# A hybrid attention and expert layer on one core: 188 tokens gathered in five parts and 324 dense (before: 184 in four and 328), query weights' low parts on GpSimd, twenty early rows, three branch products ahead

## The chip, the cores and the metric

The kernel runs on one core of a Trainium2 chip. The time is the device time of one execution in microseconds (us), from the run itself; the median of several is given, with the lowest and the highest. Each kernel is also executed once under the hardware profiler; that execution has a time of its own.

Engines are named as in the profile: PE is TensorE (PEld its weight loads), DVE is VectorE, ACT is ScalarE, POOL is GpSimd, and SP is SyncE, which here only issues DMAs. L246 is line 246 of the kernel before.

## The reference

One layer over 16 meta tokens and 512 frames of width 2048, in float32: two attention mixers, whose gated outputs are added, and then a layer of 16384 experts, of which every token uses 128.

```python
hn = rmsnorm(h, norm_mix_g)
c_q, c_kv, k_rope, q_sb, k_sb, v_sb, gate_a, gate_b = split(hn @ w_in)
y_a = mla_attention(...)                 # 8 heads, softmax, chunk-causal
y_b = stick_breaking_attention(...)      # 8 heads
h += (sigmoid(gate_a) * (y_a @ w_branch_a) + sigmoid(gate_b) * (y_b @ w_branch_b)) @ w_out

x = rmsnorm(h, norm_ffn_g)
q = (x @ w_q).reshape(tokens, 8, 2, 128)             # 8 heads, two halves
s = einsum('thcd,hcnd->thcn', q, sub_keys)           # 128 keys for each half
s1, i1 = top_k(s[:, :, 0], 16);  s2, i2 = top_k(s[:, :, 1], 16)
top_s, pos = top_k(s1[..., :, None] + s2[..., None, :], 16)   # 16 of 256 pairs
idx = i1[...] * 128 + i2[...]                        # at pos
g = softmax(top_s)
act = g * gelu(einsum('tkd,td->tk', u[idx], x))      # 128 experts a token
h += einsum('tk,tkd->td', act, v[idx])
out = rmsnorm(h, final_norm_g)[frames]
```

## The kernel before

**Products.** Every float32 product is made of three matmuls (`mm3`, L258): both operands are split into a high part (`wh`, `xh`: a copy on ACT rounded to the type fp32r) and a low part (`wl`, `xl`: the operand minus its high part, on DVE by default), and low times high, high times low and high times high are added in PSUM. `wtile` (L232) does this for a weight tile of 128 x 1024: SP loads it (`wr`, four buffers), ACT copies the high part, and DVE, or the engine given as `eng`, subtracts the low part; `wh` and `wl` have three buffers. `front(name, m, hf, eng)` is `wtile` for the weights ahead of the expert layer. `split` (L263) is the same for other operands.

**Stages**, in program order: the projections of `w_in` and the stick-breaking heads; the eight MLA heads, whose generators `mla_s`, `mla_p` and `mla_y` are run in turns by `run`, so that one head's scores, another's projections and a third's output products alternate; the branch stage, 16 columns of `wa` and `wb` products with gates, which begins by splitting the stick-breaking output `yb` into `yh_b` and `yl_b`; `wo`; the query stage (16 columns `hc`, L1125), in which each column is one half of one head's query for all 512 tokens, two weight tiles of eight products each, followed by the scores against 128 keys and the top 16 of them for four token blocks (`top16`, L917 to L921: MAX, MAX_INDEX, MATCH_REPLACE on DVE; tiles `sc`, `wk`, `lists`); the u stage (128 steps `e`, L1347, each two weight tiles of eight products); the v stage (256 blocks in the order STEPS, L1441); and the final norm.

**Dense and gathered tokens.** The expert layer is computed in two ways. For ND = 328 tokens all 16384 experts are multiplied densely: in the u stage `u` times x, GELU, and a store to DRAM (`h_d`); in the v stage these come back (`hin`), are multiplied by a gate matrix from DRAM (`gin`; `g_d`, built during the u stage from the top-16 results) and multiplied with `v`. The other 184 tokens are gathered: for each of a token's 128 experts the row of `u` or `v` is fetched by an indirect DMA of 128 rows at once, and multiplied by DVE. These come in parts, NS = 128, 32, 16, 8: the first part is one token a partition and 128 gathers long; in a part of n tokens each token holds 128 / n partitions, and n gathers do. So the parts need 128 + 32 + 16 + 8 = 184 gathers of `u` and as many of `v`, 1 MB each. The x of the parts lie in `xg`, `xgb` and, reloaded from `xr_d`, in `lists`; the sums of the v rows of a part of n tokens are spread over its partitions and are added up at the end by matmuls with a selection matrix (`select`; `acc` is the output accumulator). For the last part 16 such matmuls of 128 x 8 stand in step 5 of the v stage (L1464 to L1469).

**Rows.** `todo` lists the gathers in their order. `send` issues the next one on POOL's queue (L1052) into a buffer `row`; `row_step` (L1057) sends what its lead asks for and then does one row on DVE: a multiply with a sum for `u` (L1065, 128 x 2048), a multiply-add for `v` (L1073). A NOSYNC dependency only keeps the row behind an earlier instruction of DVE (`mark`). In the query stage one row step is made at the end of every column from the sixth on (`if hc > 4`), 11 in all; two gathers are sent at the end of column 4. In the u stage `rows_due` keeps the number of rows done at the curve PACE: (0, 11), (14, 28), (60, 97), (127.5, 200). What remains is done in the v stage by PACE_V. In the query stage there are three `row` buffers, so a gather waits for the row step three before it.

These lines set the order around the rows and the query weights:

```python
1019 NU = 200
1023 PACE = (0, 14, 60, NK - 0.5), (11, 28, 97, NU)
1128 wh, wl = wq.pop((hc, hf)) if (hc, hf) in wq else front("wq", hc, hf, G if hf else V)
1155 split(qh, ql, ps)
1189 row_step(more["lo"], 2)
```

By L1128 the low parts of a column's second weight tile are on POOL and those of the first on DVE; (0, 0), (1, 0), (1, 1) and (2, 0), loaded ahead, are on DVE and (0, 1) is on POOL. POOL runs its queue in order, so there a low part stands behind the gathers issued before it.

## Time and profile before

| | us |
|---|---|
| median of three runs | 3459.06 (3458.64 to 3461.61) |
| profiled execution, its own time | 3459.31 |
| its span (first to last instruction) | 3457.6 |
| projections and stick-breaking heads | 0 to 800 |
| MLA heads | 800 to 965 |
| branch stage, then `wo` | 965 to 1148, 1148 to 1305 |
| query stage | 1305 to 1519 |
| u stage | 1519 to 2500 |
| v stage and final norm | 2500 to 3457 |

How to read the profile: the busy line gives each engine's busy time, its share of the span and its number of instructions. Below it the span is cut into 40 slices of 86 us, and a digit is the busy share in tenths. A group of instructions reads: line, engine, operation, output <- inputs, shapes, count | busy time, mean ns of one | idle time of the engine just before these instructions, and what ended most of it. Matmuls overlap, so that their mean is longer than the time from one to the next. A row of the waits names who waited with what, for whom with what, and then the total, the count and the longest. In the timeline and in the chain the first two numbers are start and duration. "x" counts merged instructions.

### The profile page before, as it was taken

The numbers are of one execution on the slowest core, as the hardware profiler recorded it, in microseconds if no ns is written. First come the engines' busy times: TensorE is split into PE (matmuls) and PEld (weight loads), VectorE is DVE, ScalarE is ACT, GpSimd is POOL, SyncE is SP. The second block draws the span as 40 slices with busy tenths as digits, with TensorE's granted clock in tenths as the row PEclk, the third lists the DMA queues.
The fourth block names the chain that finished last, engine by engine and source line by source line (L and its number), as shares of the span: only waits on it lengthen the run. The fifth ranks groups of instructions, "written<-read, shape, count | busy, mean of one in ns | idle before, by whom it ended". The sixth has DMA issues, their size and how long they took to land.

```text
span 3457.6 us, 53380 instructions
## 1 busy us (share of the span) xinstructions
PE 3420.5 (99%) x21115; PEld 3188.2 (92%) x21115; DVE 2573.5 (74%) x3573; ACT 1427.4 (41%) x2304; POOL 776.1 (22%) x555
## 2 busy tenths in 40 slices
PE   9999999999999999999999999999999999999997
PEld 8988888887888888889999999999999999999997
DVE  5533334445754557999999988887889999999997
ACT  4233333334543223223576776774333333333333
POOL 1000000000001113322333333333213333333320
PEclk9999999999999999999999999999999999999998
DMA  5322323232144345559999999999999999999993
GB/s 171 100 98 100 98 100 100 89 101 74 62 131 143 129 143 181 204 214 367 377 389 407 405 412 412 405 401 398 403 362 375 394 408 400 402 382 399 409 381 116
DMA packets 227141, 919.94 MB, mean 266 GB/s; under 512 B 27806, under 2 KB 53518, under 8 KB 179090
## 3 DMA queue, kind: packets, MB, share of 16 engines
q1 hardware_dynamic: 134660, 466.11, 36.6%
q0 software_dynamic: 60480, 411.68, 30.0%
q10 hardware_dynamic: 31750, 38.75, 3.1%
q8 instruction: 165, 2.70, 0.3%
q14 instruction: 86, 0.70, 0.1%
HBM read 854.57 MB, written 62.91 MB: 265 GB/s over the span
## 4 chain that ended last, share of the span: by engine, by line
PE 81%; DVE 11%; DMA 4%; issue 2%; ACT 1%; SPq 0%; POOL 0%; DVEq 0%; ACTq 0%
PE ps L259 26%; PE ps L260 25%; PE ps L261 25%; DMA wr<-vb 3%; DVE wl L246 3%; DVE xg L1073 1%; DVE row L1065 1%; PE ps L1252 1%; DVE acc L1073 1%; DVE acc L1500 1%; DVE hgl L246 0%; ACT wh L245 0%; DVE hin L1337 0%; DMA row<-u,eo 0%; DVE acc L1429 0%
## 5 line engine op out<-in xcount | busy, mean ns | idle before, releaser
L245 ACT ACTIVATE wh<-wr 128x1024 fp32r<-128x1024 f32 (+1 forms) x654 | 687.8, 1053 | 1402.6 <-PE ps L261 1038.7
L246 DVE TENSOR_TENSOR wl<-wr,wh 128x1024 fp32r<-128x1024 f32 (+1 forms) x639 | 812.0, 1279 | 391.5 <-ACT wh L245 389.3
L259 PE MATMUL ps<-vah,wl 128*128 128x328 f32 x2048 | 643.8, 314 | 7.0 <-DVE wl L246 6.8
L260 PE MATMUL ps<-val,wh 128*128 128x328 f32 x2048 | 642.7, 314 | 0.0
L261 PE MATMUL ps<-vah,wh 128*128 128x328 f32 x2048 | 639.7, 312 | 0.0
L259 PE MATMUL ps<-hgh,wl 128*128 128x328 f32 (+1 forms) x1488 | 490.9, 330 | 2.8 <-DVE wl L246 2.8
L261 PE MATMUL ps<-hgh,wh 128*128 128x328 f32 (+1 forms) x1488 | 486.1, 327 | 0.0
L260 PE MATMUL ps<-hgl,wh 128*128 128x328 f32 (+1 forms) x1488 | 485.8, 326 | 0.0
L259 PE MATMUL ps<-xh,wl 128*128 128x512 f32 (+1 forms) x1376 | 468.1, 340 | 1.5 <-ACT xh L366 1.5
L260 PE MATMUL ps<-xl,wh 128*128 128x512 f32 (+1 forms) x1376 | 465.0, 338 | 0.8 <-DVE xl L367 0.8
L261 PE MATMUL ps<-xh,wh 128*128 128x512 f32 (+1 forms) x1376 | 464.9, 338 | 0.0
L259 PEld LDWEIGHTS ps<-vah,wl 128*128 128x128 f32 x2048 | 386.3, 189 | 9.5 <-DVE wl L246 9.3
L260 PEld LDWEIGHTS ps<-val,wh 128*128 128x128 f32 x2048 | 387.1, 189 | 0.0
L261 PEld LDWEIGHTS ps<-vah,wh 128*128 128x128 f32 x2048 | 386.8, 189 | 0.0
L1052 POOL DMA_INDIRECT row<-v,eo x128 | 215.5, 1684 | 481.4 <-DVE xg L1073 414.4
L1073 DVE SCALAR_TENSOR_TENSOR xg<-row,act,xg 128x2048 f32<-128x2048 f32 x127 | 297.5, 2343 | 1.2 <-DMA row<-v,eo 1.1
L1065 DVE SCALAR_TENSOR_TENSOR row<-row,xg 128x2048 f32<-128x2048 f32 x128 | 292.1, 2282 | 4.8 <-DMA row<-u,eo 4.8
L259 PEld LDWEIGHTS ps<-hgh,wl 128*128 128x128 f32 x1488 | 280.1, 188 | 14.6 <-DVE wl L246 3.4
L261 PEld LDWEIGHTS ps<-hgh,wh 128*128 128x128 f32 x1488 | 280.1, 188 | 11.7 <-issue 0.2
L260 PEld LDWEIGHTS ps<-hgl,wh 128*128 128x128 f32 x1488 | 280.4, 188 | 10.9
L259 PEld LDWEIGHTS ps<-xh,wl 128*128 128x128 f32 x1376 | 258.6, 188 | 30.2 <-ACT xh L366 3.0
L260 PEld LDWEIGHTS ps<-xl,wh 128*128 128x128 f32 x1376 | 259.1, 188 | 29.1 <-DVE xl L367 1.7
(517 smaller groups left out, 6057.6 us busy)
## 6 DMA issues: line engine op xcount, KB each, us to landing
wr<-ut SPq DMA_DIRECT2D x256, 512.0 KB, 9.4
wr<-vb SPq DMA_DIRECT2D x256, 512.0 KB, 8.0
wr<-front SPq DMA_DIRECT2D x238, 512.0 KB, 3.3
g_d<-gb POOLq DMA_DIRECT2D x42, 512.0 KB, 10.9
gin<-g_d SPq DMA_DIRECT2D x32, 672.0 KB, 7.4
h_d<-hb ACTq DMA_DIRECT2D x128, 164.0 KB, 8.3
hin<-h_d SPq DMA_DIRECT2D x32, 656.0 KB, 8.9
gates<-gt ACTq DMA_DIRECT2D x32, 256.0 KB, 2.0
```

The costliest lines, as they stand in the source:

```text
L245: more["last"] = S.activation(hi[:, s], r, AF.Copy)
L246: sub = (eng or V).tensor_sub(lo[:, s], r, hi[:, s].bitcast(F32))
L259: T.matmul(ps, wl, xh, start=start, stop=False)
L260: T.matmul(ps, wh, xl, start=False, stop=False)
L261: T.matmul(ps, wh, xh, start=False, stop=stop)
L1052: G.indirect_dma_start(out=row, out_offset=None, in_=a[src], in_offset=bass.IndirectOffsetOnAxis(ap=eos[part][:, k:k + 1], axis=0))
L1065: ins = V.scalar_tensor_tensor(row, row, 1.0, xs[part], ALU.mult, ALU.mult, accum_out=w)
L1073: ins = V.scalar_tensor_tensor(y, row, w, y, ALU.mult, ALU.add)
L1252: T.matmul(bank[:, o:o + P], ohs[q % 4][:, 1, :, t], wos[:, q % 4, c, :, t], start=c == 1, stop=c == 0)
L1500: mark = V.tensor_add(acc[:, c, :ND], acc[:, c, :ND], ps[:, :ND])
```

## The change

The token split changes from 128 + 32 + 16 + 8 gathered and 328 dense to 128 + 32 + 16 + 8 + 4 and 324; with it go a fifth part's lists, sums and selection (16 more matmuls of 128 x 4, now at steps 2 and 6 of the v stage), NU 200 becomes 210, and the order of the v rows in `todo` changes. Beside that:

- the low parts of both weight tiles of a query column are made on POOL, but for the tiles loaded ahead, which stay as they were, and (15, 1), which goes to DVE: 27 on POOL instead of 15;
- from column 7 on a second row step is made in every column, behind the issue of the second weight tile, so that 20 rows are done ahead of the u stage; a fourth `row` buffer (`row0`) lies in the score pool; the row steps are marked by the previous column's query split, and their lead is 3;
- PACE becomes (0, 20), (14, 38), (60, 108), (127.5, 210);
- `branch_ahead`: the splits of `yb` are made during the last two MLA heads into the buffers of `cqh`, `ckh`, `cql`, `ckl`, and the `wb` products of columns 0, 1 and 2 during the last head; the branch stage then takes their PSUM banks from `ready`;
- the transposes at column 4 alternate between two PSUM banks.

```diff
...
@@ -37,7 +38,7 @@
 TA = SEQ - P
-NS = 128, 32, 16, 8
+NS = 128, 32, 16, 8, 4
 NB = sum(NS[1:])
...
@@ -290,7 +291,7 @@
     xn_d = dp.tile([NB, D], F32, name="xn_d")
-    xr_d = dp.tile([2, P, D], F32, name="xr_d")
+    xr_d = dp.tile([3, P, D], F32, name="xr_d")
     h_d = dp.tile([NG, P, GRP, ND], F32, name="h_d")
@@ -797,6 +798,24 @@
     run(mla_s(0), mla_p(1))
+    AHEAD = 3
+    ready = {}
+
+    def branch_ahead():
+        bh, bl = ([lp.tile([P, 4, n], F32R, name=x, tag=t)[:, :, :SEQ] for t, n in ((f"cq{p}", SEQ), (f"ck{p}", LEN))]
+                  for x, p in (("ybh", "h"), ("ybl", "l")))
+        for h in range(H):
+            split(bh[h // 4][:, h % 4], bl[h // 4][:, h % 4], yb[:, h])
+            yield
+        for m in range(AHEAD):
+            wh, wl = front("wb", m)
+            ps = ready[m] = ps_tile()
+            for k in range(8):
+                s = slice(k * P, (k + 1) * P)
+                mm3(ps, wh[:, s], wl[:, s], bh[k // 4][:, k % 4], bl[k // 4][:, k % 4], k == 0, k == 7)
+                if k % 2:
+                    yield
+
     for h in range(H):
@@ -804,7 +823,10 @@
             values(1)
-        run(*([mla_s(h + 1)] if h + 1 < H else []), *([mla_p(h + 2)] if h + 2 < H else []), mla_y(h))
+        if h == H - 2:
+            ahead = branch_ahead()
+        run(*([mla_s(h + 1)] if h + 1 < H else []), *([mla_p(h + 2)] if h + 2 < H else []), mla_y(h),
+            *([ahead] if h == H - 1 else [islice(ahead, 9)] if h == H - 2 else []))
     stage.close()
@@ -828,11 +850,14 @@
             SP.dma_start(gt, gates[gi, m])
-            wh, wl = front(name, m)
-            ps = ps_tile()
-            for k in range(8):
-                s = slice(k * P, (k + 1) * P)
-                mm3(ps, wh[:, s], wl[:, s], yh_[:, k], yl_[:, k], k == 0, k == 7)
+            if gi and m in ready:
+                ps = ready.pop(m)
+            else:
+                wh, wl = front(name, m)
+                ps = ps_tile()
+                for k in range(8):
+                    s = slice(k * P, (k + 1) * P)
+                    mm3(ps, wh[:, s], wl[:, s], yh_[:, k], yl_[:, k], k == 0, k == 7)
             sg = S.activation(gt, gt, AF.Sigmoid)
@@ -1016,19 +1041,22 @@
     slots = [[(i, k) for k in range(n)] for i, n in enumerate(NS)]
-    NU = 200
+    NU = 210
+    EARLY = 20
     todo = [("u", *s) for i in range(3) for s in slots[i]]
-    todo += [("v", *s) for s in slots[0][:NU - NR]] + [("u", *s) for s in slots[3]]
-    todo += [("v", *s) for s in slots[3] + slots[0][NU - NR:NU - NR + 44] + slots[2] + slots[0][NU - NR + 44:] + slots[1]]
-    PACE = (0, 14, 60, NK - 0.5), (11, 28, 97, NU)
+    todo += [("v", *s) for s in slots[0][:10]] + [("u", *s) for s in slots[3]]
+    todo += [("v", *s) for s in slots[0][10:NU - NR]] + [("u", *s) for s in slots[4]]
+    todo += [("v", *s) for s in slots[4] + slots[0][NU - NR:NU - NR + 16] + slots[3]
+             + slots[0][NU - NR + 16:NU - NR + 52] + slots[2] + slots[0][NU - NR + 52:] + slots[1]]
+    PACE = (0, 14, 60, NK - 0.5), (EARLY, 38, 108, NU)
     PACE_V = (0, 64, 488), (0, 20, 2 * NR - NU)
     OWN = NU - 16
-    xs, ys = [xg, xgb, lists, lists], [xg, xgb]
+    xs, ys = [xg, xgb, lists, lists, lists], [xg, xgb]
     acts = [act] + [actb[:, a:b] for a, b in cuts]
...
     rcols = [rcol] + [rcolb[:, j:j + 1] for j in range(len(cuts))]
-    gs = {"sent": 0, "done": 0, "pool": None, "gated": False, "six": None, "third": False, "x": 1, "rows": None, "vi": None}
+    gs = {"sent": 0, "done": 0, "pool": None, "gated": False, "six": None, "third": False, "x": 1, "rows": None, "vi": None, "early": None}
@@ -1038,12 +1066,14 @@
         if gs["vi"] is None:
-            tag = "rows"
+            tag = "rows" if n % 4 < 3 or n > EARLY - 4 else "row0"
         elif n < OWN and gs["six"] is not None:
...
             tag = ("rows", "hin")[n % 5 % 2] if n < OWN else "rows"
-        if tag != "rows":
+        if tag == "row0":
+            row = gs["early"].tile([P, D], F32, name="row", tag=tag, bufs=1)
+        elif tag != "rows":
             row = gs["vi"].tile([P, D], F32, name="row", tag=tag)
@@ -1073,9 +1103,10 @@
         gs["done"] += 1
-        if gs["done"] == sum(NS[:3]) + 8:
-            gs["x"] = 3
-            SP.dma_start(lists, xr_d[1])
+        for nxt, at in ((3, sum(NS[:3]) + 4), (4, sum(NS[:4]) + 14)):
+            if gs["done"] == at:
+                gs["x"] = nxt
+                SP.dma_start(lists, xr_d[nxt - 2])
         if src == "u" and k == NS[part] - 1:
...
@@ -1125,7 +1157,9 @@
             for hf in range(2):
-                wh, wl = wq.pop((hc, hf)) if (hc, hf) in wq else front("wq", hc, hf, G if hf else V)
+                wh, wl = wq.pop((hc, hf)) if (hc, hf) in wq else front("wq", hc, hf, V if hc == 15 and hf else G)
+                if hf and hc > 6:
+                    row_step(more["dve"], 3)
                 for k in range(8):
@@ -1152,7 +1186,7 @@
                 S.dma_start(xn_d, xgb[:NB])
-            split(qh, ql, ps)
+            more["dve"] = split(qh, ql, ps)
             late.append((hc, qh, ql))
@@ -1160,20 +1194,21 @@
                 T.transpose(pt_[:, :P], rh_[:, TA:], ident)
+                pt2 = ps_tile()
+                T.transpose(pt2[:, :P], rh_[:, TA - P:TA], ident)
                 for j, (t, n) in enumerate(zip(BC[1:], NS[1:])):
                     V.tensor_copy(rr[:, j].rearrange("p (t r) -> p t r", r=P // n), rh_[:, t, None].to_broadcast([P, n, P // n]))
-                    T.transpose(pt_[:, (j + 1) * P:(j + 2) * P], rr[:, j], ident)
+                    T.transpose((pt_, pt2)[j % 2][:, (j // 2 + 1) * P:(j // 2 + 2) * P], rr[:, j], ident)
                 V.tensor_copy(rcol, pt_[:, :1])
-                pt2 = ps_tile()
-                T.transpose(pt2[:, :P], rh_[:, TA - P:TA], ident)
                 V.tensor_copy(rcol2, pt2[:, :1])
                 for j in range(len(NS) - 1):
-                    V.tensor_copy(rcolb[:, j:j + 1], pt_[:, (j + 1) * P:(j + 1) * P + 1])
+                    o = (j // 2 + 1) * P
+                    V.tensor_copy(rcolb[:, j:j + 1], (pt_, pt2)[j % 2][:, o:o + 1])
             if hc:
...
                 copies(xgb, BO[1], NS[1])
-            if hc in (9, 12):
+            if hc in (9, 12, 15):
                 copies(xr_d[hc // 3 - 3], BO[hc // 3 - 1], NS[hc // 3 - 1])
@@ -1186,7 +1221,8 @@
             if hc > 4:
-                row_step(more["lo"], 2)
+                row_step(more["dve"], 3)
+        assert gs["done"] == EARLY
         ahead = u_products(0)
@@ -1391,7 +1427,7 @@
     select = ap2.tile([P, NB], F32, name="select")
-    last_sums = ap2.tile([P, KC, NS[3]], F32, name="last_sums")
+    last_sums = [ap2.tile([P, KC, n], F32, name="last_sums") for n in NS[3:]]
     SP.dma_start(select, a["select"])
@@ -1461,16 +1497,21 @@
                 residual(i - 3, acc[:, i - 3, :TA], slice(0, TA))
-            if (i, qi) == (5, 0):
-                assert NU + NS[3] < gs["done"] and gs["sent"] < NU + NS[3] + 44
+            if (i, qi) in ((2, 4), (6, 4)):
+                part = 4 if i == 2 else 3
+                first, last = [todo.index((src, part, k)) for src, k in (("v", 0), ("v", NS[part] - 1))]
+                follow = [x for x in range(last, len(todo)) if todo[x][1] in (2, 3) and x > last][0]
+                assert last < gs["done"] and gs["sent"] <= follow, (gs["done"], gs["sent"], last, follow)
                 ps = ps_tile()
+                m = NS[part]
                 for c in range(KC):
-                    T.matmul(ps[:, c * NS[3]:(c + 1) * NS[3]], acc[:, c, TA:], select[:, cuts[2][0]:], start=True, stop=True)
-                V.tensor_copy(last_sums, ps[:, :KC * NS[3]].rearrange("p (c t) -> p c t", t=NS[3]))
+                    T.matmul(ps[:, c * m:(c + 1) * m], acc[:, c, TA:], select[:, cuts[part - 1][0]:cuts[part - 1][1]], start=True, stop=True)
+                V.tensor_copy(last_sums[part - 3], ps[:, :KC * m].rearrange("p (c t) -> p c t", t=m))
             if (i, qi) == (20, 0):
-                assert gs["done"] > NU + NS[3] + 44 + NS[2]
+                assert gs["done"] > todo.index(("v", 2, NS[2] - 1))
                 gather_sums(lambda c: acc[:, c, TA:], BC[2], select[:, cuts[1][0]:cuts[1][1]])
-                V.tensor_add(acc[:, :, BC[3]], acc[:, :, BC[3]], last_sums)
+                for b, sums in zip(BC[3:], last_sums):
+                    V.tensor_add(acc[:, :, b], acc[:, :, b], sums)
             if qi in (0, 3) and 21 <= i < 29:
```

On DVE, in the query stage around the end of column 8's query (`pql` is the low part of the query, `wl` that of a weight, `row` a gathered row, `lists` and `wk` belong to the top 16), there stood before:

```order
L921 MAX_INDEX lists<-lists,wk 128x8
L919 MATCH_REPLACE wk<-lists,sc 128x128
L920 MAX lists<-wk 128x8
L921 MAX_INDEX lists<-lists,wk 128x8
L265 TENSOR_TENSOR pql<-ps,pqh 128x512
L246 TENSOR_TENSOR wl<-wr,wh 128x1024
L1065 SCALAR_TENSOR_TENSOR row,act<-row,xg 128x2048
L917 MAX lists<-sc 128x8 x2
```

and now:

```order
L946 MAX_INDEX lists<-lists,wk 128x8
L1095 SCALAR_TENSOR_TENSOR row,act<-row,xg 128x2048
L944 MATCH_REPLACE wk<-lists,sc 128x128
L945 MAX lists<-wk 128x8
L946 MAX_INDEX lists<-lists,wk 128x8
L944 MATCH_REPLACE wk<-lists,sc 128x128
L945 MAX lists<-wk 128x8
L946 MAX_INDEX lists<-lists,wk 128x8
L266 TENSOR_TENSOR pql<-ps,pqh 128x512
L1095 SCALAR_TENSOR_TENSOR row,act<-row,xg 128x2048
L942 MAX lists<-sc 128x8 x2
```

The low part of the weight is gone from DVE, and a second row step stands among the top-16 instructions ahead of the query's low part.

On POOL, from the end of `wo` into the query stage (`xn` are loads of x for the dense tokens, `row<-u,eo` the gathers), there stood before:

```order
L246 TENSOR_TENSOR wl<-wr,wh 128x1024
L1102 DMA xn<-ht_d 128x328 x16
L246 TENSOR_TENSOR wl<-wr,wh 128x1024 x5
L1052 DMA row<-u,eo 128x2048 x3
L246 TENSOR_TENSOR wl<-wr,wh 128x1024
L1052 DMA row<-u,eo 128x2048 x3
L246 TENSOR_TENSOR wl<-wr,wh 128x1024
L1052 DMA row<-u,eo 128x2048 x2
```

and now:

```order
L247 TENSOR_TENSOR wl<-wr,wh 128x1024
L1134 DMA xn<-ht_d 128x324 x16
L247 TENSOR_TENSOR wl<-wr,wh 128x1024 x10
L1082 DMA row<-u,eo 128x2048 x4
L247 TENSOR_TENSOR wl<-wr,wh 128x1024
L1082 DMA row<-u,eo 128x2048 x2
L247 TENSOR_TENSOR wl<-wr,wh 128x1024 x2
L1082 DMA row<-u,eo 128x2048
L247 TENSOR_TENSOR wl<-wr,wh 128x1024
L1082 DMA row<-u,eo 128x2048 x2
```

Twice as many low parts stand ahead of the first gathers, and behind them low parts and gathers alternate more closely.

On PE, in the last MLA head (`th`, `tl_` are the transposed probabilities, `vnh` and `vnl` the values, `cst,pt` transposes), there stood before:

```order
L781 MATMUL ps<-th,vnl 128x512
L782 MATMUL ps<-th,vnh 128x512
L772 MATMUL ps<-cst,pt 128x128 x3
L783 MATMUL ps<-tl__8130,vnh 128x512
L781 MATMUL ps<-th,vnl 128x512
L782 MATMUL ps<-th,vnh 128x512
L783 MATMUL ps<-tl__8139,vnh 128x512
```

and now:

```order
L782 MATMUL ps<-th,vnl 128x512
L783 MATMUL ps<-th,vnh 128x512
L784 MATMUL ps<-tl__8163,vnh 128x512
L773 MATMUL ps<-cst,pt 128x128 x3
L260 MATMUL ps<-ybh,wl 128x512
L261 MATMUL ps<-ybl,wh 128x512
L262 MATMUL ps<-ybh,wh 128x512
L260 MATMUL ps<-ybh,wl 128x512
L261 MATMUL ps<-ybl,wh 128x512
L262 MATMUL ps<-ybh,wh 128x512
L782 MATMUL ps<-th,vnl 128x512
```

Six branch products now stand between the transposes of one block and the output products of the block before.

4 lines of the change are left out of this document (3 added, 1 removed).

## The prediction

> **What bounds the kernel now.** I read the page first, its busy line and its slices, then the busy times by stage, the matmul groups by shape, and last the waits of TensorE.
>
> ```profile
> PE 3420.5 (99%) x21115; PEld 3188.2 (92%) x21115; DVE 2573.5 (74%) x3573; ACT 1427.4 (41%) x2304; POOL 776.1 (22%) x555
> PE   9999999999999999999999999999999999999997
> DVE  5533334445754557999999988887889999999997
> DMA  5322323232144345559999999999999999999993
> ```
>
> PE is busy all the way, but a mean over stages hides that from slice 16 on DVE and the DMA engines are full too. The stage table (start:end, then busy us and instructions of PE, PEld, DVE, ACT, POOL, then granted clock, DMA share, GB/s) separates them.
>
> ```profile
> 1396.00:1432.00 36.00, 35.58 (x172) 29.36 (x171) 30.96 (x112) 9.20 (x12) 14.85 (x11) 1.00 0.86 309
> 1432.00:1544.00 112.00, 109.72 (x574) 94.34 (x572) 109.83 (x414) 29.65 (x39) 24.60 (x17) 1.00 0.51 174
> 1544.00:1700.00 156.00, 155.92 (x1032) 155.28 (x1033) 155.28 (x299) 65.96 (x95) 41.28 (x30) 0.99 0.97 371
> 1700.00:1825.00 125.00, 123.85 (x899) 121.84 (x899) 121.95 (x218) 86.81 (x203) 39.89 (x32) 1.00 1.00 387
> 1825.00:1950.00 125.00, 125.00 (x899) 123.47 (x898) 122.72 (x183) 85.23 (x194) 46.19 (x33) 1.00 1.02 407
> 1950.00:2500.00 550.00, 550.00 (x3923) 544.55 (x3921) 453.95 (x467) 335.40 (x731) 190.60 (x135) 1.00 1.02 406
> 2600.00:3400.00 800.00, 798.91 (x5325) 797.90 (x5324) 744.24 (x636) 266.27 (x249) 256.88 (x146) 1.00 0.98 386
> ```
>
> From 1432 to 1825 us, the second half of the query and score stage and the first forty experts or so of the u stage, DVE is idle for 2.17 + 0.72 + 3.05 = 5.9 us of 393. From 1950 on it has room again (454 of 550, 744 of 800). So there are two regimes: until about 1825 PE and DVE both stand at their limit, and work added to DVE moves the end; behind that PE alone sets the pace. The waits of PE between 1390 and 1950 us and the chain around the longest say the same.
>
> ```profile
> PE ps L259 <- DVE wl L246: 2.8, 2, 2.4
> 1542.59 0.31 DVE wk L919 x2
> 1542.90 1.14 DVE wl L246
> 1544.08 0.53 PE ps L259
> 1785.98 1.14 DVE wl L246
> 1787.12 0.38 DVE row L1065
> ...
> 1822.38 0.48 DVE L1279 MEMSET gb<- 128x512 f32 x1 [2.19 <-DMA g_d<-gb]
> ...
> 1544.60:1547.90 3.30, 3.30 (x15) 3.30 (x14) 3.30 (x7) 1.66 (x2) 0.24 (x1) 0.54 0.84 307
> ```
>
> At 1544 PE waits 2.4 us for a low part that DVE reaches only after top-16 work (`wk`) and rows; the chain runs through DVE again at 1786. The last two rows, of DVE's timeline and of the stage table, I use below: DVE's one longer wait, and the clock of 0.54 that follows the halt at 1544 for some 3.3 us.
>
> **The change part by part.**
>
> *Four dense columns fewer.* The dense products are 128x328 and become 128x324.
>
> ```profile
> L259 PE MATMUL ps<-vah,wl 128*128 128x328 f32 x2048 | 643.8, 314 | 7.0 <-DVE wl L246 6.8
> L259 PE MATMUL ps<-hgh,wl 128*128 128x328 f32 x1232 | 388.7, 315 | 2.4 <-DVE wl L246 2.4
> L259 PE MATMUL ps<-hgh,hgl 128*128 128x328 f32 x816 | 258.6, 317 | 1.1 <-DVE hgl L246 1.1
> 1100.00:1150.00 50.00, 50.00 (x222) 41.43 (x221) 22.75 (x22) 17.04 (x21) 5.16 (x4) 1.00 0.39 131
> 3150.00:3200.00 50.00, 50.00 (x336) 50.00 (x335) 47.36 (x40) 17.48 (x16) 15.87 (x10) 1.00 1.00 395
> ```
>
> The means of 314 ns count overlapping matmuls twice, so I take the pitch: 222 of 512 columns in 50 us are 225.2 ns each, 336 of 328 columns are 148.8. That is 76.4 ns for 184 columns, 0.415 ns a column, 1.66 ns for four. With three lines each there are 6144 products in the u stage and 6144 in the v stage; if PE sets the pace everywhere, 12288 x 1.66 = 20.4 us go. Where DVE sets it they go for nothing, and that holds to about 1825 us, which is expert 40 (68 rows are done there, by the old pace at e = 40). Left are 88 x 48 + 6144 = 10368 products, **-17.2 us**. The gate products fall from 656 to 648 128x128 matmuls, under half a microsecond: -0.4.
>
> *Query low parts to GpSimd, 20 early rows.* The rows of the groups that carry it, DVE over 1432 to 1544 us, POOL over the run, and the flight of the gathers in the query stage:
>
> ```profile
> L1065 DVE SCALAR_TENSOR_TENSOR row<-row,xg 128x2048 f32<-128x2048 f32 x9 | 20.5, 2281 | 0.0
> L246 DVE TENSOR_TENSOR wl<-wr,wh 128x1024 fp32r<-128x1024 f32 x11 | 13.4, 1214 | 0.2 <-ACT wh L245 0.2
> L246 POOL TENSOR_TENSOR wl<-wr,wh 128x1024 fp32r<-128x1024 f32 x15 | 39.0, 2598 | 51.4 <-ACT wh L245 48.4 <-issue 2.8
> row<-u,eo POOLq DMA_INDIRECT x19, 6.5
> ```
>
> Thirteen low parts leave DVE and one comes, (15, 1). Four of the thirteen lie before the first row, where DVE had time; that relief buys nothing. Behind it DVE loses 8 x 1.21 = 9.7 us. It gains nine row steps in the same columns, and by the new pace it is 10.6 rows ahead of the old one at e = 40 (78.6 against 68): 10.6 x 2.28 = 24.2 us. Net **+14.5 us of DVE work** in the stretch where DVE has 5.9 us left, of which 2.2 us are one wait for a gate buffer's transfer and the rest gaps between instructions. The bounds are 14.5 - 5.9 = 8.6 us when all gaps are used, and 14.5 plus what GpSimd's extra subtractions block (below). I take +12 for the time at e = 40, nearer to no usable gap, since PE's halt at 1544 shows no reserve there. On GpSimd 27 low parts instead of 15 are 12 x 2.6 = 31 us in a stage where it is mostly idle. But each gather stands ahead of a low part in its queue and waits for a row's buffer, so a late row step on DVE holds the gather, the low part behind it and then PE. That adds no second delay, as DVE is the one that is late; it only moves part of PE's halt into the query stage. The row buffers go from three to four, and the gather of row n waits for step n-4; at two rows a column that is two columns (25 us) before use, against a median of 6.5 us in flight, so rows aren't late.
>
> One cost is in the trace only by example. The same 128x32 operations on DVE, with and without a low part running on GpSimd:
>
> ```profile
> 1453.81 2.98 DVE L993 SCALAR_TENSOR_TENSOR e__11788<-ef 128x32 f32<-128x32 f32 x1
> 1454.34 2.40 POOL L246 TENSOR_TENSOR wl<-wr,wh 128x1024 fp32r<-128x1024 f32 x1
> 1456.92 0.16 DVE L994 CAST eo<-e__11788 128x32 int32<-128x32 f32 x1
> 1503.68 0.17 DVE L993 SCALAR_TENSOR_TENSOR e__12259<-ef 128x32 f32<-128x32 f32 x1
> 1503.97 2.66 DVE L994 CAST eo<-e__12259 128x32 int32<-128x32 f32 x1
> 1504.20 2.39 POOL L246 TENSOR_TENSOR wl<-wr,wh 128x1024 fp32r<-128x1024 f32 x1
> ```
>
> 2.98 against 0.17 us: a DVE operation that meets GpSimd's subtraction ends with it. The change has 12 more of them, so 0 to 12 x 2.4 = 28.8 us of blocking; removed low parts and shared gathers bring some back. A low part starts right behind a row step's gather, and the next instructions on DVE are top-16 ones, of about 0.28 us, that show no stretching; I take +1 inside the +12. The Trainium skill, page "SBUF — State Buffer", section "Who interferes with whom", states that a VectorE instruction with two SBUF inputs and a GpSimd instruction that reads SBUF exclude each other for the whole instruction. The trace agrees for `e_` above; it shows no row step overlapped by such a subtraction. By that rule the row step itself (`row` and `xg`, both in SBUF) would be blocked too, which speaks against the move; the rival below prices it from the rows.
>
> *Branch products ahead.* Three of the 16 `wb` products move into the last heads, to lie in PE's waits:
>
> ```profile
> 959.74 0.41 PE L772 MATMUL ps<-cst,pt 128*128 128x128 f32 x2 [1.01 <-DVE pt L755]
> 960.73 0.50 PE L781 MATMUL ps<-th,vnl 128*128 128x512 f32 x1 [0.58 <-ACT th L264]
> 966.22 1.89 DVE L265 TENSOR_TENSOR yl_b<-yb,yh_b 128x512 fp32r<-128x512 f32 x3
> ```
>
> The 72 products cost the same in either place. What can go is PE's waiting in the last head, 1.01 + 0.58 us shown, somewhat more with the thin 16-row products beside it: 0 to -3. Against it stand eight more splits of `yb` (0.63 us each, 5 us) on DVE between the maxima and scalings of the last two heads, ahead of `pt`, which PE waits for: up to +2. I take **-1.5**.
>
> *The fifth part.* Its sums need 16 more selection matmuls, alone on PE:
>
> ```profile
> 2631.30 3.63 PE L1468 MATMUL ps<-select,acc 128*128 128x8 f32 x32
> ```
>
> Each is recorded twice and the pitch is not set by the 8 columns, so four columns cost the same: **+3.6 us** on PE's path, bounded by 1.8 (if columns counted) and 5.3 (if PE restarts at half clock for 3.3 us, as it does after 1544). Eight more rows in all, but the dense stages carry 190 + 166 against 189 + 168, so their DMA and DVE work stays; the extra 9 MB fall into a stage with a DMA share of 0.51. The list reloads on SP come five rows behind the last reader and don't hold the weights queued behind them. With PE 1.1% faster the margins of the v stage shrink: +1 for short waits, 0 to 3.
>
> **Sum**, against the profiled execution (3459.31 us around a span of 3457.6; the three runs' median is 3459.06): -17.2 - 0.4 + 12 - 1.5 + 3.6 + 1 = -2.5. **Prediction 3456.8 us**, no change: a measurement of this kernel tells about 0.2% (6.9 us) from none, so 3452.1 to 3466.0 is the same.
>
> **The rivals.**
>
> *DVE's lateness is absorbed* (3446 us). Condition: the gaps and the waits on `pql` in the query stage can be used, and PE reaches e = 40 no more than 3 us late or with the columns' gain. 3459.3 - 20.4 - 0.4 + 5 - 1.5 + 3.6 + 1 = 3446.6. For it: DVE's idle 5.9 us, and 8.6 as the lower bound of the delay. Against it: PE halted for DVE at 1544 already. Chance 0.23.
>
> *GpSimd's subtractions block the row steps* (3471 us, slower). Place: query columns 7 to 15, where two rows and two low parts share 12.5 us. Price: 2.4 us for a step that meets one fully; half of that for each of 12 is 14.4 us on DVE's path, on top of the +12. It decides from 0.8 us each on (9 us more). For it: the 2.98 above. Against it: by the order of the queues a low part starts behind a step, not ahead of it. Chance 0.17.
>
> *The DMA engines become the bound* (3465 us). A share of 1.00 to 1.02 from 1700 to 2500 leaves nothing for a faster PE; if half the columns' gain is lost there and in the v stage, 3456.8 + 8.6 = 3465. Against it: no PE wait on a transfer between 1950 and 2500. Chance 0.10.
>
> **How the numbers follow.** The forecast (3452 to 3462) has 0.50. Range: 3446 to 3470, from the first rival to the second; about a tenth is left out on each side. Faster: 0.23 and a small part of the forecast's low end, 0.27. Slower: most of 0.17 and some of the DMA case, 0.19. Same: 0.54.
>
> **What would show it.** Right: u and v products at a pitch of about 147.2 ns in the v stage; PE halts of 10 us or more for `wl` between the fifteenth query column and the first experts; PE some 10 us later than before at e = 40, relative to the start of the query stage; then steady gain. The second rival would show as row steps well over 2.28 us on average in the query stage; the third as waits of ACT or PE on `wr<-ut` and `wr<-vb`; the first as a query stage that ends no later than before. I am wrong if DVE's busy time there doesn't rise by some 10 us.

## The result and the profile after

The changed kernel takes 3478.44 us (median of five runs, 3473.42 to 3481.97) against 3459.06 (five runs, 3452.12 to 3461.67). The ratio is 1.006 with a 95% interval of 1.0047 to 1.0074: slower by 0.6%, where 3456.8 us and no change were forecast, and outside the range that was given (3446 to 3470). The profiled execution took 3478.44 us around a span of 3476.4, 18.8 us more than the span before.

From the start times of the first product of each column `q`, expert `u` and v block in the two traces one can say where PE falls behind. The table gives after minus before in us; `v 0` is the start of the v stage, and the last column is the last v block.

| wo | q 4 | q 5 | q 12 | u 0 | u 3 | u 20 | u 25 | u 60 | v 0 | last v |
|---|---|---|---|---|---|---|---|---|---|---|
| -2.9 | -2.8 | +1.9 | +2.4 | +19.1 | +27.0 | +24.2 | +29.5 | +29.7 | +27.7 | +18.3 |

So the branch products bring 2.9 us. Then the kernel loses 4.7 us in query column 4 and 25.1 from column 5 to expert 3. It gains 2.8 up to expert 20, loses 5.3 between experts 20 and 25 and 0.2 up to expert 60, and gains 2.0 in the rest of the u stage. The v stage brings 9.4.

The page of the changed kernel, its busy line and two rows of slices:

```profile
PE 3419.8 (98%) x21140; PEld 3183.4 (92%) x21140; DVE 2589.1 (74%) x3584; ACT 1428.7 (41%) x2303; POOL 805.5 (23%) x575
PE   9999999999999999989999999999999999999997
DMA  5332222232144345669999999999999999999993
```

And its stage table (start:end, busy us and instructions of PE, PEld, DVE, ACT, POOL, then clock, DMA share, GB/s):

```profile
1432.00:1544.00 112.00, 99.09 (x455) 81.38 (x455) 110.35 (x350) 23.71 (x31) 44.71 (x27) 0.94 0.57 200
1544.00:1700.00 156.00, 149.93 (x989) 148.93 (x988) 151.82 (x331) 57.25 (x69) 48.93 (x31) 0.98 0.94 362
1700.00:1825.00 125.00, 121.27 (x874) 119.44 (x873) 120.72 (x205) 84.92 (x201) 42.13 (x30) 0.99 0.98 374
```

Between 1432 and 1544 us PE was busy for 109.72 us before and now for 99.09, at a clock of 0.94; DVE is as full as before (110.35 against 109.83) with fewer instructions (350 against 414). The same stretch of PE's waits (engine, tile, line <- what it waited for: total, times, longest), from 1400 to 1565 us:

```profile
PE ps L260 <- DVE wl L247: 8.7, 3, 4.1
PE ps L260 <- POOL wl L247: 5.3, 1, 5.3
PE ps L260 <- DVE pql L266: 1.2, 2, 0.9
```

**The row steps are longer.** The row steps of DVE between 1390 and 1544 us, before and after (busy us, mean ns of one):

```profile
L1065 DVE SCALAR_TENSOR_TENSOR row<-row,xg 128x2048 f32<-128x2048 f32 x14 | 32.0, 2284 | 4.5 <-DMA row<-u,eo 4.5
```

```profile
L1095 DVE SCALAR_TENSOR_TENSOR row<-row,xg 128x2048 f32<-128x2048 f32 x21 | 62.3, 2969 | 2.2 <-DMA row<-u,eo 2.2
```

Seven steps more in this window would be 16.0 us, but the group grew by 30.3; 14.3 us (62.3 - 21 x 2.284) are stretching. Before, no step was stretched. The 14.3 us lie in six of the 21 steps, which took 3.2 to 5.5 us. Each of the six overlaps one or two subtractions on POOL and is longer than 2.28 us by the time of that overlap, to within 0.2 us; in none of the runs below was a row step longer than 2.6 us without such an overlap. The timeline of the changed kernel at column 12, where PE's longest wait is (start, duration; x counts merged instructions; in brackets the idle time before and its end):

```profile
1478.86 0.94 POOL L1082 DMA_INDIRECT row<-u,eo  x1 [4.50 <-DVE wk L944]
1479.82 4.66 POOL L247 TENSOR_TENSOR wl<-wr,wh 128x1024 fp32r<-128x1024 f32 x2
1481.20 5.43 DVE L1095 SCALAR_TENSOR_TENSOR row<-row,xg 128x2048 f32<-128x2048 f32 x1
1482.22 0.80 PE L260 MATMUL ps<-hgh,wl 128*128 128x512 f32 x1 [5.31 <-POOL wl L247]
```

POOL's queue holds a gather, and behind it two low parts, one of which PE already waits for. The gather waits until a row step on DVE has freed its buffer (1478.6 us), the two low parts follow without a gap, and the next row step, which DVE reaches at 1481.20, takes 5.43 us: it ends 2.2 us after the second low part does. So the row step delays the low part and the low part delays the row step, in turns. The Trainium skill, page "SBUF — State Buffer", section "Who interferes with whom", has this rule (a VectorE instruction with two SBUF inputs and a GpSimd instruction that reads SBUF exclude each other), and the trace now shows it for the row step itself.

The traces have the other case too: a row step that begins first keeps POOL waiting. Here is one of e8_one_row (below), with one row step a column:

```profile
1415.62 2.28 DVE L1099 SCALAR_TENSOR_TENSOR row<-row,xg 128x2048 f32<-128x2048 f32 x1
1416.01 4.16 POOL L247 TENSOR_TENSOR wl<-wr,wh 128x1024 fp32r<-128x1024 f32 x1 [3.10 <-ACT wh L246]
```

The row step takes its usual time, and the subtraction 4.16 us instead of 2.4. Mostly the one that begins later pays, but not always: at 1404.21 us in the same run a row step that began 0.5 us ahead of a subtraction took 5.03 us.

**A load held up by a copy.** The 4.7 us at column 4 are of another kind. SP's timeline and ACT's there:

```profile
1354.95 0.33 SPq L1217 DMA_DIRECT2D wr<-front  x1
...
1368.45 1.06 ACT L265 ACTIVATE skh<-wr 128x1024 fp32r<-128x1024 f32 x1 [15.53 <-DMA wr<-front]
```

And the busy times of a window in which ACT waits:

```profile
1360.00:1367.50 7.50, 7.50 (x40) 6.31 (x39) 0.00 (x0) 0.00 (x0) 0.00 (x0) 1.00 0.24 99
```

The key tile is issued at 1354.95 and lands at 1368.4, while the DMA engines are busy to 0.24: about four of sixteen. Ahead of it on SP's queue stand two copies `xr_d<-xn_d`, where one stood before; the new one, for the fifth part, spreads 4 rows of x over 128 and has 4 as its outer dimension.

**Small loads in a row.** At 1693 us SP issues eight loads of spread indices and gates (`eob`, `gwb`), with one u weight between the sixth and the seventh. Before there were six, three at 1633 and three at 1664. SP's wait ahead of the first of them in the changed kernel, and then their neighbours from SP's and DVE's timelines:

```profile
SPq L960 <- DMA eob_d<-er: 7.3, 1, 7.3
```

```profile
1692.78 0.34 SPq L960 DMA_DIRECT2D eob<-eob_d  x1
...
1696.82 0.45 SPq L244 DMA_DIRECT2D wr<-ut  x1
1697.32 0.72 SPq L960 DMA_DIRECT2D eob<-eob_d  x1
1701.47 0.32 SPq L960 DMA_DIRECT2D gwb<-gwb_d  x1
...
1704.28 0.29 DVE L1271 TENSOR_SCALAR more_oh<-ps 128x128 f16<-128x128 f32 x1 [6.59 <-ACT gr_last L1269]
```

The first load reads what a store (`eob_d<-er`, issued at 1683.73) has just written, and SP's queue stands for 7.3 us until that has landed; then six loads take 4.0 us ahead of the weight, which lands 6.0 us after its issue. ACT and then DVE (6.6 us) stand still, and PE halts for 3.7 us at 1708. The wait for the store was there before as well (6.7 us), with three loads behind it, which took 1.4 us.

### The profile page after: what moved, and what is told of

It is laid out like the page before. It is cut to its first block, busy times and chain, and to the rows that moved or that the text cites. A ratio compares the mean times of both kernels' runs of the same rounds, so it can differ in the third digit from the quotient of the medians.

```text
span 3476.4 us, 53485 instructions
## 1 busy us (share of the span) xinstructions
PE 3419.8 (98%) x21140; PEld 3183.4 (92%) x21140; DVE 2589.1 (74%) x3584; ACT 1428.7 (41%) x2303; POOL 805.5 (23%) x575
## 3 DMA queue, kind: packets, MB, share of 16 engines
q0 software_dynamic: 61632, 420.03, 30.2%
## 4 chain that ended last, share of the span: by engine, by line
PE 72%; DVE 17%; DMA 5%; issue 4%; ACT 1%; SPq 0%; POOL 0%; DVEq 0%; ACTq 0%; POOLq 0%
PE ps L260 23%; PE ps L262 22%; PE ps L261 22%; DVE row L1095 3%; DVE wl L247 3%; DMA wr<-vb 2%; DMA wr<-ut 2%; DVE xg L1103 1%; DVE hgl L247 1%; PE ps L1288 1%; DVE wk L944 1%; DMA wr<-front 1%; DVE acc L1103 1%; ACT wh L246 0%; DVE acc L1541 0%
## 5 line engine op out<-in xcount | busy, mean ns | idle before, releaser
L247 DVE TENSOR_TENSOR wl<-wr,wh 128x1024 fp32r<-128x1024 f32 (+1 forms) x627 | 793.2, 1273 | 393.2 <-ACT wh L246 382.3
L260 PE MATMUL ps<-vah,wl 128*128 128x324 f32 x2048 | 639.0, 312 | 4.6 <-DVE acc L1541 2.3
L262 PE MATMUL ps<-vah,wh 128*128 128x324 f32 x2048 | 639.1, 312 | 0.0
L261 PE MATMUL ps<-val,wh 128*128 128x324 f32 x2048 | 638.6, 312 | 0.0
L260 PE MATMUL ps<-hgh,wl 128*128 128x324 f32 (+1 forms) x1488 | 494.1, 332 | 22.5 <-DVE wl L247 14.4
L262 PE MATMUL ps<-hgh,wh 128*128 128x324 f32 (+1 forms) x1488 | 488.7, 328 | 0.0
L261 PE MATMUL ps<-hgl,wh 128*128 128x324 f32 (+1 forms) x1488 | 488.2, 328 | 0.0
L1082 POOL DMA_INDIRECT row<-v,eo x128 | 196.2, 1533 | 504.5 <-DVE xg L1103 401.2
L1095 DVE SCALAR_TENSOR_TENSOR row<-row,xg 128x2048 f32<-128x2048 f32 x128 | 306.1, 2392 | 2.2 <-DMA row<-u,eo 2.2
L262 PEld LDWEIGHTS ps<-hgh,wh 128*128 128x128 f32 x1488 | 282.9, 190 | 12.2 <-issue 0.2
L261 PEld LDWEIGHTS ps<-hgl,wh 128*128 128x128 f32 x1488 | 283.2, 190 | 11.1
```

Source lines behind the costliest of these rows:

```text
L247: sub = (eng or V).tensor_sub(lo[:, s], r, hi[:, s].bitcast(F32))
L260: T.matmul(ps, wl, xh, start=start, stop=False)
L261: T.matmul(ps, wh, xl, start=False, stop=False)
L262: T.matmul(ps, wh, xh, start=False, stop=stop)
L1082: G.indirect_dma_start(out=row, out_offset=None, in_=a[src], in_offset=bass.IndirectOffsetOnAxis(ap=eos[part][:, k:k + 1], axis=0))
L1095: ins = V.scalar_tensor_tensor(row, row, 1.0, xs[part], ALU.mult, ALU.mult, accum_out=w)
```

## The experiments

The theory: POOL's subtractions stretch the row steps, and two row steps a column are more than DVE has room for with it; the copy and the index loads are two further losses. Times of one kernel differ by 10 us and more between executions here (the kernel before: 3453 to 3466 in 21 runs), so losses are read from the place where they arise in the profiled execution, by the same table as above (us against the profiled execution of before), beside the medians. A place doesn't repeat exactly either: e4_no_ahead and e5_index_act have the query stage of the change, and lose 29.2 and 27.9 us from column 5 to expert 3 where the change loses 25.1, and 2.3 and 2.1 us in column 4 where it loses 4.7.

| | wo | q 4 | q 5 | q 12 | u 0 | u 3 | u 20 | u 25 | u 60 | v 0 | last v |
|---|---|---|---|---|---|---|---|---|---|---|---|
| e1_copy | -2.3 | -2.3 | -2.2 | -2.9 | +10.0 | +17.7 | +14.8 | +20.6 | +21.3 | +19.3 | +9.6 |
| e2_lows | -2.8 | -2.8 | -1.6 | +9.0 | +16.3 | +22.7 | +18.7 | +23.5 | +24.1 | +22.1 | +12.6 |
| e3_one_row | -3.0 | -3.0 | -0.6 | -1.3 | -1.3 | -0.7 | +3.0 | +12.8 | +18.4 | +23.6 | +19.7 |
| e4_no_ahead | +0.2 | +0.3 | +2.6 | +6.1 | +22.9 | +31.8 | +27.7 | +38.5 | +37.9 | +35.9 | +30.2 |
| e5_index_act | -2.8 | -2.8 | -0.7 | +2.8 | +19.5 | +27.2 | +24.2 | +24.0 | +24.9 | +25.7 | +14.3 |
| e8_one_row | -2.6 | -2.6 | -2.5 | -3.1 | -3.1 | -2.6 | -2.0 | -2.1 | -2.0 | +0.8 | +10.9 |
| e9_no_lo | -2.1 | -2.1 | +1.0 | +0.3 | +8.4 | +17.1 | +13.2 | +17.6 | +17.6 | +15.6 | +7.6 |
| e11_lows_one | -0.9 | -0.9 | -0.8 | +0.2 | +1.7 | +3.7 | +5.9 | +5.7 | +2.8 | +3.7 | +11.0 |
| e12_16 | -0.7 | -0.7 | -0.6 | -1.2 | +6.2 | +9.8 | +10.5 | +10.4 | +10.3 | +16.3 | +9.9 |
| e13_16_210 | -2.6 | -2.7 | -2.6 | -3.2 | +4.1 | +7.7 | +8.5 | +8.4 | +9.3 | +12.8 | +9.4 |
| e14_between | -2.8 | -2.7 | -2.6 | -3.3 | -2.7 | +4.0 | +4.8 | +4.6 | +5.8 | +8.4 | +5.2 |
| e15_before_pool | -3.1 | -3.1 | -3.1 | -3.8 | -3.8 | -3.2 | -1.6 | -1.3 | -3.1 | -2.7 | -2.7 |

**e1_copy.** The fifth part's copy in another order, the rest as changed:

```diff
+        if n == 4:
+            SP.dma_start(dst.rearrange("(t r) d -> r t d", r=P // n), xn_d[None, t0:t0 + n, :].to_broadcast([P // n, n, D]))
+            return
         SP.dma_start(dst, xn_d[t0:t0 + n, None, :].to_broadcast([n, P // n, D]))
```

> Theory (copy): the DRAM-to-DRAM copy that spreads the four x rows of the fifth part runs on few of the 16 DMA engines (a DMA share of about 0.2 for 13 us) and holds the pieces of the weight load behind it; with its descriptors in another order (over the 32 repeats first, 4 rows inside) the load lands within about 4 us, ACT's wait of 15.5 us for the key tile goes, and PE's halt of 3.2 us at query column 4 with its half clock goes: 4.7 us less, about 3473.7 against 3478.4. Rival (the load is late for another reason, such as the queue of SP or a weight buffer): the halt stays and the time is 3478.

3472.1 us (3469.11 to 3476.0). Column 4 loses nothing now (-2.3 to -2.2), and the key tile is there in time; the rival falls. A window of e1_copy around its copies:

```profile
1351.50:1356.00 4.50, 4.50 (x26) 3.83 (x26) 3.23 (x18) 1.93 (x3) 2.40 (x1) 1.00 0.73 271
```

The DMA share around the copies is 0.73 instead of 0.24. The Trainium skill, page "DMA: Bandwidth & Descriptors", section "Rules for kernel authors", says that an outermost dimension of size c below 16 confines a DMA to at most c engines; with c = 4 the share of 0.24 agrees. The loss in column 4 varies: in the five other runs that keep the copy as in the change it is 1.2 to 3.1 us, and in the six with the other order 0.1 at most. At expert 3 the gain is 9.3 us, more than the 4.7 of the copy. The row steps' stretching is 8.8 us here (59.0 - 22 x 2.284, in the window of the groups above), 5.5 less than in the change, though the query code behind the copy is the same.

**e2_lows.** The low parts as before, 20 early rows:

```diff
-front("wq", hc, hf, V if hc == 15 and hf else G)
+front("wq", hc, hf, G if hf else V)
```

> The query low parts as before (second half of a column on POOL, first on DVE); 20 early rows stay. Theory (GpSimd's subtraction holds the row steps): the 14.5 us by which 21 row steps are longer than 2.28 us between 1396 and 1544 us fall to under 5, DVE has 9.7 us of subtractions more, and the time stays within 4 us of 3478 or falls. Rival (only DVE's own work counts): the row steps' lengths hardly matter, DVE has about 10 us more to do, and the time rises to about 3488.

3475.68 us (3471.83 to 3477.24). The row steps' group between 1390 and 1544 us:

```profile
L1095 DVE SCALAR_TENSOR_TENSOR row<-row,xg 128x2048 f32<-128x2048 f32 x21 | 54.5, 2594 | 2.3 <-DMA row<-u,eo 2.3
```

The stretching is 6.5 us instead of 14.3 (not under 5). DVE's own subtractions came back, and from column 5 to expert 3 it loses 24.3 us where the change loses 25.1. What POOL stretches and what DVE would do itself are about the same here; the rival's 3488 falls.

**e3_one_row.** One row step a column, 11 early rows, low parts on POOL:

```diff
-                if hf and hc > 6:
-                    row_step(more["dve"], 3)
-    EARLY = 20
+    EARLY = 11
-    PACE = (0, 14, 60, NK - 0.5), (EARLY, 38, 108, NU)
+    PACE = (0, 14, 60, NK - 0.5), (EARLY, 30, 102, NU)
```

> One row step a query column as before (11 early rows; PACE 11, 30, 102, 210), all low parts on POOL as in the change. Blocking theory: half as many row steps meet a subtraction, so some 7 us of stretching and 20 us of row work leave the query stage; expert 3 comes 15 us or more earlier than in the change and the time falls to about 3462. Rival (the two-row columns aren't the cause, the halts come from the late gathers and buffers): under 5 us less, 3474 or more.

3476.77 us (3468.5 to 3489.81): by the time, the rival's number. By the place, the theory's: expert 3 starts 27.7 us earlier than in the change, and the query stage loses nothing but the copy. All of it comes back later: 9.8 us between experts 20 and 25 (the place of the index loads), 5.6 to expert 60 and 5.2 to the v stage. The rows moved out of the query stage are late in the u stage.

**e4_no_ahead.** The generator of branch products isn't run:

```diff
-            *([ahead] if h == H - 1 else [islice(ahead, 9)] if h == H - 2 else []))
+            *[])
```

> Without the branch products ahead and their splits. All theories: wo starts 2.9 us later than in the change (as before), and nothing else differs: 3481.2. If the splits' buffers or PSUM banks held something up, less than that.

3486.31 us (3483.0 to 3489.73). `wo` starts 3.1 us later than in the change, as expected; from there the profiled execution loses 1.7 us more than the change by expert 3 and 5.5 more between experts 20 and 25. The median is 7.9 us above that of the change, where 2.8 were expected. The row steps' stretching is 15.9 us (61.6 - 20 x 2.284), 1.6 more than in the change. What else lies beyond the 3.1 us at `wo` wasn't traced to a cause.

**e5_index_act.** The index loads on ACT's queue at experts 60 and 61:

```diff
-                SP.dma_start(to[:, o:o + n], src[t0:t0 + n].rearrange("t (r k) -> (t r) k", r=P // n))
+                ld = S.dma_start(to[:, o:o + n], src[t0:t0 + n].rearrange("t (r k) -> (t r) k", r=P // n))
+                tc.add_manual_dep(ld.ins, more["last"].ins.name, NOSYNC, reason="not before its expert")
```

> The change, with the eight small loads of the spread indices and gates (eob, gwb; one pair more than before) on ACT's queue at experts 60 and 61, where they stood in a row on SP's queue at 1693 us between two u weights. Theory (index loads): a u weight behind them lands late, DVE idles 6.6 us and PE halts 4.0 us at 1708 with its half clock; without them PE loses nothing between experts 20 and 25: 5.3 us less, about 3473. Rival (DVE's backlog made that halt): the loss between experts 20 and 25 stays over 3 us.

3478.65 us (3473.95 to 3483.53). At the place the theory holds: from expert 20 to 25 it loses nothing (+24.2, +24.0), and DVE's wait of 6.6 us is gone. The later kernels with moved loads lose nothing there either, and the five others that keep them on SP's queue lose 4.4 to 10.8 us. The move takes away SP's wait for the store and the row of loads together; which of the two counts more wasn't tried. In the median nothing is gained: the expected time was a miss. Between experts 60 and 80, behind the moved loads, the profiled execution loses 1.9 us.

**e9_no_lo.** Eight of POOL's subtractions are left out, the high part being used twice; DVE's own work and its rows are those of the change:

```diff
-front("wq", hc, hf, V if hc == 15 and hf else G)
+front("wq", hc, hf, V if hc == 15 and hf else G, copy=6 < hc < 15 and not hf)
...
+            if copy:
+                return
             sub = (eng or V).tensor_sub(lo[:, s], r, hi[:, s].bitcast(F32))
```

> The change without the low parts of the first weight tile of query columns 7 to 14 (eight subtractions on POOL left out; PE uses the high part twice there). Blocking theory: the row steps' stretching in the query stage falls from 14.5 us to 5 or less and expert 3 starts 8 to 14 us earlier than in the change. Rival (the stretched steps cost nothing, DVE's 20 row steps by themselves are late): stretching falls, but expert 3 starts less than 4 us earlier.

3466.84 us (one run). The row steps:

```profile
L1097 DVE SCALAR_TENSOR_TENSOR row<-row,xg 128x2048 f32<-128x2048 f32 x22 | 55.1, 2504 | 1.6 <-DMA row<-u,eo 1.6
```

55.1 - 22 x 2.284 = 4.9 us of stretching instead of 14.3: 9.4 less. Expert 3 starts 9.9 us earlier than in the change (17.1 against 27.0), and 9.0 of that lie between column 5 and expert 3 (16.1 lost against 25.1); the rival falls. This run alone doesn't separate the row steps from the low parts that are left out: PE's wait for a low part of POOL falls too, from 5.3 to 1.2 us. But the change and three runs in which no subtraction is left out agree with it. All five in this table have 20 early rows and the low parts on POOL (us):

| | stretching | lost from column 5 to expert 3 | difference |
|---|---|---|---|
| e9_no_lo | 4.9 | 16.1 | 11.2 |
| e1_copy | 8.8 | 19.9 | 11.1 |
| the change | 14.3 | 25.1 | 10.8 |
| e5_index_act | 15.7 | 27.9 | 12.2 |
| e4_no_ahead | 15.9 | 29.2 | 13.3 |

A microsecond of stretching goes with about a microsecond on PE's path. That is what decides it for the blocking.

**e8_one_row** and **e11_lows_one.** Copy and index loads mended, one row step a column, 200 rows by the end of the u stage; e11_lows_one shares the low parts as before:

```diff
-    NU = 210
+    NU = 200
-    PACE = (0, 14, 60, NK - 0.5), (EARLY, 38, 108, NU)
+    PACE = (0, 14, 60, NK - 0.5), (EARLY, 28, 97, NU)
```

> The change with one row step a column (11 early rows, 200 by the end of the u stage, PACE as before), all low parts on POOL, the copy of the fifth part's x in the other order and the index loads on ACT's queue. Theory (the loss is the two-row columns, the copy and the index loads): expert 3 starts about 3 us earlier than in the kernel before, the u stage keeps that and the v stage gains some 7 us: about 3446 to 3450, faster than before. Rival (fewer columns give nothing, or DVE's work comes back in the u and v stages): 3458 or more.

> As e8_one_row, but with the query low parts shared between DVE and POOL as before. Blocking theory: DVE has 13 subtractions more (15.7 us, 9.7 behind the first row) and some 6 us less stretching, so expert 3 starts 0 to 5 us later than in e8_one_row and the time is 0 to 5 us higher. Rival (one row step a column leaves POOL's subtractions harmless and DVE with reserve): no difference at expert 3.

e8_one_row: 3466.55 us (3461.1 to 3470.49; ratio 1.0009 to 1.0027). The query stage and most of the u stage are as expected, 2 to 3 us ahead of before to expert 60, but the v stage loses 10.1 us instead of gaining 7, by PE's waits for DVE (2500 to 3400 us):

```profile
PE ps L260 <- DVE wl L247: 10.1, 9, 5.1
PE ps L260 <- DVE acc L1543: 7.0, 3, 4.1
```

It has 176 rows in the v stage where the kernel before had 168 and the change 166. e11_lows_one: 3472.67 us (3467.35 to 3477.28); from column 5 to expert 3 it loses 4.5 us where e8_one_row loses nothing. Their stretching is 0.0 (13 steps of 2283 ns) and 4.6 us (15 of 2596 ns). So with one row a column the low parts are better on POOL, stretching included. e11_lows_one also loses 4.5 us against the kernel before, which has the same low parts and as many row steps there. What else in the change costs that (the row steps' mark and lead, the fifth part's small work) wasn't tried.

**e12_16** and **e13_16_210.** A second row step in columns 7 to 11 only; 206 and 210 rows by the end of the u stage:

```diff
-                if hf and hc > 6:
+                if hf and 6 < hc < 12:
-    EARLY = 20
+    EARLY = 16
```

> The change with the copy and the index loads mended as in e1_copy and e5_index_act, the second row step in columns 7 to 11 only (16 early rows instead of 20; columns 12 to 15 lost most of the time), 206 rows by the end of the u stage (170 left for the v stage, where e8_one_row had 176 and the change 166). Theory (the rows fit before column 12 and not behind it; the v stage has room for some 168 rows): the u stage starts 2 to 6 us later than in e8_one_row, the v stage gains 6 to 9 us instead of losing 10: 3450 to 3456. Rival (any second row step beside POOL's low parts is late at once): expert 3 starts over 8 us later than in e8_one_row, and the time is 3462 or more.

> As e12_16, with 210 rows by the end of the u stage (PACE 16, 33, 104, 210) and 166 in the v stage, as in the change. Theory: the v stage gains 9 us as in the change, but the u stage behind expert 60 loses 2 to 6 us to its four further rows: within 3 us of e12_16. Rival (the u stage has room behind expert 60, as its DVE share of 454 in 550 us suggests): no loss there and 2 to 3 us faster than e12_16.

3462.9 (3455.07 to 3469.57) and 3469.7 us (3465.4 to 3471.41). The halt at column 12 is there in both; expert 3 is 12.4 and 10.3 us later than in e8_one_row, as the rival had it. In e12_16 the u stage starts 9.3 us later than in e8_one_row, where 2 to 6 were expected, and loses 6.0 us behind expert 60; the v stage gains 6.4, as expected. e12_16 at column 12:

```profile
1475.75 4.66 POOL L247 TENSOR_TENSOR wl<-wr,wh 128x1024 fp32r<-128x1024 f32 x2
...
1477.13 7.75 DVE L1099 SCALAR_TENSOR_TENSOR row<-row,xg 128x2048 f32<-128x2048 f32 x1
```

In e13_16_210 the u stage loses 3.5 us behind expert 60, and the v stage brings 3.4, not 9; it was to be within 3 us of e12_16 and is 6.8 slower.

**e14_between.** The second row step in columns 9, 10, 13 and 14:

```diff
-                if hf and 6 < hc < 12:
+                if hf and hc in (9, 10, 13, 14):
-    EARLY = 16
+    EARLY = 15
```

> The change with copy and index loads mended as in e12_16, the second row step only in columns 9, 10, 13 and 14 (15 early rows), away from the columns in which DVE also ranks pairs (8, 12 and behind 15); 206 rows by the end of the u stage. Theory (a second step is late where it meets pair ranking, since POOL's low parts already stretch that): no halt over 2 us at column 12, where e12_16 had 5.2, and expert 3 starts at most 4 us later than in e8_one_row; 3457 to 3462. Rival (the number of steps counts, not the place): four of e12_16's five further steps leave most of its halt, some 4 us at column 12, and expert 3 starts 7 us or more later than in e8_one_row.

3463.86 us (3460.73 to 3470.2). No halt up to column 15 (-3.3 throughout), where e12_16 with one step more lost 7.4 at column 12: the place does matter. The stretching is 4.7 us (45.8 - 18 x 2.284) against 13.6 in e12_16 (54.7 - 18 x 2.284). But expert 3 is 6.6 us later than in e8_one_row, between the two expectations: behind column 15 PE waits twice for low parts on DVE, 3.1 us each (1532 and 1544 us), the second time while DVE ranks pairs.

**e15_before_pool.** The kernel before with the low parts on POOL and the branch products ahead alone:

```diff
-front("wq", hc, hf, G if hf else V)
+front("wq", hc, hf, V if hc == 15 and hf else G)
...
+            if gi and m in ready:
+                ps = ready.pop(m)
```

> The kernel before with two parts of the change alone: the query low parts on POOL and the three branch products ahead; 184 gathered tokens and one row step a column. Theory (both parts are gains by themselves, and the loss is in the fifth part's rows): wo starts 2.8 us earlier, the u stage some 3 us earlier than before, and the rest is as before: 3454 to 3456 against 3458, at the limit of what can be told. Rival (the low parts on POOL are themselves a loss through stretched row steps): 3460 or more.

3456.25 us (3451.12 to 3460.24, 11 runs) against 3458.52 (3453.15 to 3466.3, 21 runs), ratio 0.9995 (0.9986 to 1.0004). The profiled execution is ahead all the way, by 1.3 to 3.8 us; the time alone can't tell it from no change. It is the fastest kernel of the study; no version with the fifth part beat the kernel before.

## Why the prediction was wrong

- **Row steps and POOL's subtractions: the step that failed.** The prediction took +1 us for GpSimd's blocking, inside a +12, because a low part starts behind a row step and meets only top-16 operations. With one row a column that nearly holds (3.9 us of stretching in e15_before_pool, 38.2 - 15 x 2.284, and 4.6 in e8_one_row). With two, the next row step comes 2 to 3 us behind the end of the first, while two queued low parts run for 4.7 us. The blocking was 14.3 us, in six of 21 steps, and over five runs the loss on PE's path follows it about one for one (the table under e9_no_lo).
- **The second rival** had the mechanism and the size (14.4 us) and ended at 3471; it was given 0.17. That the size agrees is partly luck: it counted half of 2.4 us for each of 12 subtractions, and there were six steps with 0.9 to 3.3 us each.
- **DVE's work: right in kind.** From column 5 to expert 3 the change loses 25.1 us. Without the second rows it loses nothing there (e3_one_row: -0.6 and -0.7), and with 9.4 us less stretching it loses 16.1 (e9_no_lo). So the rest, about 11 us, goes with the further rows. But the +12 was set for expert 40. There the change is 29.9 us behind, counted from the start of the query stage; less the stretching and the two missing terms below (14.3, 4.7 and 5.3) some 6 us are left, half of the +12. The rows at expert 40 were misread by one, 78.6 and 68 for 77.6 and 67.0; their difference of 10.6 is right.
- **That the moved GpSimd work adds no second delay: wrong.** "It only moves part of PE's halt" overlooked that a late low part on POOL holds back the next row step as well. How much of the loss is the row step held by the low part, and how much the low part held by the gather ahead of it in POOL's queue, is open: no run puts the low parts ahead of the gathers.
- **Two terms were missing.** The copy of the fifth part (4.7 us; e1_copy) and the index loads (5.3 us; e5_index_act) weren't in the sum; the other runs that keep them lost 1.2 to 3.1 and 4.4 to 10.8 us there. The prediction weighed the reloads of the x lists on SP but neither the copy that feeds them nor the loads of the spread indices, though the change adds to both.
- **Four columns: right in the v stage, half in the u stage.** The v stage was to gain 10.2 us less 3.6 for the selection and 1 for waits, and it gained 9.4 in all, partly since halts of before at 2530 to 2565 us are mostly gone. The fifth part's 16 selection matmuls took 4.67 us, inside the bounds of 1.8 and 5.3. Behind expert 60 the u stage was to gain 68 x 48 x 1.66 ns = 5.4 us and gained 2.0. The matmuls in 50 us of each, first u and then v, of the changed kernel, and in the u window before:

```profile
2300.00:2350.00 50.00, 50.00 (x368) 49.38 (x366) 40.82 (x47) 35.98 (x87) 17.05 (x14) 1.00 1.02 412
3150.00:3200.00 50.00, 50.00 (x339) 50.00 (x338) 45.31 (x39) 16.86 (x16) 12.73 (x8) 1.00 0.99 390
```

```profile
2300.00:2350.00 50.00, 50.00 (x368) 49.24 (x367) 41.69 (x46) 36.03 (x84) 18.46 (x13) 1.00 1.02 394
```

  In the v window there were 336 before: nothing gained in the u window (its 368 hold gate matmuls too), 0.9% in the v window. No PE wait on a transfer shows there, so this isn't the DMA rival as it was put; the cause wasn't tried and stays open.
- **Branch products: right, too small.** -1.5 was forecast, with a bound of -3; 2.9 us were measured, and e4_no_ahead gives 3.1 of them back at `wo`.
- **By the signs set down:** PE's halts for low parts between 1524 and 1600 us came to 12.5 us (9.4 for `wl`, 3.1 for `hgl`), where 10 or more were said, and in the v window above the pitch is 147.5 ns (50 us by 339), where 147.2 was said. DVE's busy time from column 5 to expert 3 rose by 27.6 us (155.91 to 183.46), where some 10 were said. Expert 40 came 29.9 us later, counted from the start of the query stage, where "some 10 us" was said, and row steps were well over 2.28 us on average: the sign of the second rival.
